# Differential attention with its outputs in two PSUM banks in turn, two casts in ten on ScalarE, and dense bias tables in layer 0

## The chip, the cores and the metric

The kernel is one program on one core of a Trainium2 chip. The metric is the device time of the whole program in microseconds (us), the median of three runs. A core has five engines that run at the same time and wait for each other through semaphores: TensorE (PE in the profile; its weight loads are PEld), VectorE (DVE), ScalarE (ACT), GpSimd (POOL) and SyncE (SP), whose queue issues nearly all transfers here. Each engine and each queue takes its instructions strictly in the order in which the program holds them, so an instruction that waits holds up all that stands behind it. TensorE runs at one of two clocks, 1.2 or 2.4 GHz; the profile's rows give the granted clock as a share of the higher one.

## What is computed

Two transformer layers over 1024 latent tokens (a 16 x 64 grid) and 256 context tokens, width 1024, all in 32-bit numbers. The parts that the change touches are these two.

```python
# layer 0, heads 0 to 7: neighbourhood attention with a bias by relative position
bias = jnp.take(col_bias, row_off, axis=1)
s_win = einsum(q_r, k_win) * scale + bias
p = softmax(concatenate([s_win, s_ctx]))
...
# layer 1, 8 heads of two maps each: differential attention
s1 = einsum('bhqd,bhkd->bhqk', a1, k1) * scale
s2 = einsum('bhqd,bhkd->bhqk', a2, k2) * scale
p = softmax(s1) - lam * softmax(s2)
o = einsum('bhqk,bhkd->bhqd', p, v)
y = merge_heads(rms_norm(o, subln_gain) * (1.0 - lambda_init)) @ w_out
```

Every layer also has six vectors of shift, scale and gate (`ada_params`): a vector of 1024 conditioning values times a 1024 x 6144 matrix, for the latent and for the context tokens.

## The kernel before

Each 32-bit matmul operand is split into a high and a low part (`hi`, `lo`), and a product is three matmuls (`mm3`, L181 to L183). Names in the rows: `psm` is a PSUM tile of a projection, `psq` one of the small PSUM tiles for maxima and sums, `pst` scores, `psv` a head's output.

**The projections of layer 0** (about 175 to 474 us in the trace). First the values for ten token groups, twice (L181 to L183 with `vwh`), then eight chunks `ch` of queries and keys, each 72 matmuls (`project`), whose results go through PSUM and are stored to HBM as high and low parts (`qh`, `ql`, `kh`, `kl`). Three things are laid between them:

- `maxima`: the largest score of every query of every head, which the later softmax subtracts. Each step is a matmul (L432) and a maximum on VectorE (L406, L410). A budget (`early`) lets 200 steps be recorded among the projections; the rest are recorded in the attention stage.
- `ada_acc` and `ada_sum`: eight loads of 512 KB (`aw`) for one of the six vectors, sixteen multiply-adds on VectorE into two accumulators (L210, L214), and then 16 one-column matmuls on TensorE (L235) that add up the accumulators over partitions: sixteen rows of the profile for each accumulator, since each 32-bit matmul shows as two. There are three such sets here; the sum of one frees the two accumulators for the next.
- `tables`: for each pair of heads and each of two orientations, the bias rows are loaded, GpSimd adds a mask (L631), and the result is stored to the HBM tensor `sk`. Each row of 127 values is copied for all 64 columns, and `skew` later reads the table from `sk` with a stride that is one less than its row, so that column c sees the window that begins at 63 - c. The pieces are 8 and 7 rows high and use the same three buffers (`aw`) as the loads of `ada_acc`.

The order on each engine is made by a scheduler, which follows the order of recording and a priority. What is recorded under `later()` has a lower priority: it is put behind other work that could go at the same time. All `ada_acc` sets and all `tables` here are recorded under it. What the scheduler takes to be early is a forecast, not a measured time.

**Attention of layer 0** (474 to 914 us) sums its scores with table rows loaded from `sk` (`key_table`, L877 adds them) and works through heads 8 to 15 and then 0 to 7.

**Differential attention** (2510 to 2815 us): 8 heads, two halves of 512 queries each, ten key chunks `kc` in a half. For one chunk TensorE makes two maps of scores (four matmuls, L1318 and L1319), ScalarE takes two exponentials (L1323, L1324), VectorE makes the difference (L1327) and its high part (L1328, the cast), and GpSimd or VectorE the low part (L1329). Six chunks later TensorE multiplies with the values: three matmuls into the half's output `po` (`pv`, L1290 to L1292). After the tenth chunk ScalarE copies `po` to SBUF (L1300) and squares it, and three chunks into the next half `gain` sums the squares over partitions with one matmul (L1248), takes the reciprocal root (`rsqrt`, L310 to L314) and scales the output. PSUM has eight banks, and all are taken:

```python
pst = ps("t", 3, 1024)        # 3 x 2 banks: scores
po = ps("v", VB1)             # 1 bank: output of a half
gain1(o, sq, None, qmt())     # 1 bank ("q"): sums of squares
```

The rest (output projections, feed-forward parts, projections of layer 1) is left as it is, apart from `rsqrt`, which every norm calls.

Of the kernel before, what the change touches and what calls it, by code (L numbers as in the profile page):

```python
# [23 lines left out]
NFF = 22  # L24
EPS = 1e-6
GW = 64
RPW = 127
RPN = 15 * RPW
# [6 lines left out]
QB1, VB1, LAG1 = 1, 1, 6  # L35
FAR1 = (0,1,2,3,4,5,6,7)
FARS, FARE, FARQ = 27, 108, .3
T5 = [8]
# [11 lines left out]


@with_exitstack
def kernel(ctx: ExitStack, tc: tile.TileContext, xT, cond, ada_w, ada_b, win0, wv0, wout0, rp, rpf, qg, kg,
                       win1, wv1, wout1, wg, wu, wd, lamv, subln, fgain, cosT, sinT, consts, cmT, cmQ, out):
    nc = tc.nc
    f = lambda ap: ap.bitcast(F32)
# [75 lines left out]
    sk = [dram([8, 64 * RPN + 2048], f"sk{i}") for i in range(2)]  # L132

    def small_operands():
        nc.sync.dma_start(slt, subln)
# [13 lines left out]
        nc.vector.tensor_scalar(slt, slt, 1.0 - LAMBDA_INIT, None, op0=ALU.mult)  # L149

    def skew(i, h, dr0, n):
        o = 63 + dr0 * RPW
        v = sk[i][h, o : o + 64 * (RPN - 1)].rearrange("(c n) -> c n", c=64)
        return v[:, : n * RPW].rearrange("c (u y) -> c u y", y=RPW)[:, :, :GW]


    pq = [None]
# [140 lines left out]
    def later():  # L298

        return tc.high_priority(-LATER)  # L300


    def rsqrt(pool, src, w, scale, bufs=None):

        if pool is None:
            a = wpool.tile([P, 1024], F32, tag="wh", bufs=4, name=nm("rs"))
            y, s = a[:, :w], a[:, 512 : 512 + w]
        else:
            y, s = (pool.tile([P, 512], F32, tag="tmp", bufs=bufs, name=nm("rs"))[:, :w] for _ in range(2))
        after_table(nc.scalar.activation(y, src, AF.Ln, bias=eps, scale=scale))  # L310
        last_ln[0] = after_table(nc.scalar.activation(y, y, AF.Exp, scale=-0.5))
        nc.scalar.activation(s, y, AF.Square, scale=math.sqrt(0.5 * scale))
        nc.vector.scalar_tensor_tensor(s, src, EPS / scale, s, op0=ALU.add, op1=ALU.mult)
        nc.vector.scalar_tensor_tensor(y, s, 1.5, y, op0=ALU.subtract, op1=ALU.mult, reverse0=True)  # L314
        return y

    def sumsq_add(pool, ssq, x, first, tag=("tmp", 512, 8), eng=None):
# [167 lines left out]
    with sbuf("hp0", 8) as hp, sbuf("a10", 8) as ap:  # L485
# [118 lines left out]
        for g in range(2):  # L604
# [15 lines left out]
        cmt = ap.tile([P, 2, RPW], F32, tag="cmt", bufs=1, name="cmt")  # L620

        def tables(i, h):

            for d0, d1 in ((0, 8), (8, 15)):
                n = d1 - d0
                T = ap.tile([P, 8, RPW], F32, tag="aw", bufs=3, name=nm("sk"))[:, 0:n, :]
                T2 = T.rearrange("p u y -> p (u y)")
                for j in range(2):
                    src = (rpf, rp)[i][h + j : h + j + 1, d0 * RPW : d1 * RPW].to_broadcast([64, n * RPW])
                    nc.sync.dma_start(T2[64 * j : 64 * j + 64], src)  # L630
                nc.gpsimd.tensor_add(T, T, cmt[:, i : i + 1, :].to_broadcast([P, n, RPW]))  # L631
                for j in range(2):
                    dst = sk[i][h + j, : 64 * RPN].rearrange("(c n) -> c n", c=64)[:, d0 * RPW : d1 * RPW]
                    nc.sync.dma_start(dst, T2[64 * j : 64 * j + 64])

        mpool = None
        tabs8 = [(i, h) for h in range(0, 8, 2) for i in range(2)]
# [77 lines left out]
        for ch in range(8):  # L715
            w = load_wchunk(win0[ch])
            hi, lo = t5(tpool), t5(tpool)
            for b, c0, cw, _ in BLK0:
                pst = mmt()[:, :cw]
                project(pst, w, hh[b], hl[b])  # L720
                early(VSHARE + (1 - VSHARE) * (ch * 1280 + c0 + cw) / 10240)
                put_plain(pst, hi[:, c0 : c0 + cw], lo[:, c0 : c0 + cw], 0.125 if ch < 4 else None)
            r = slice(P * (ch % 4), P * (ch % 4) + P)
            q = nc.gpsimd if ch > 6 else nc.sync
            q.dma_start((qh0, kh0)[ch // 4][r], f(hi))
            q.dma_start((ql0, kl0)[ch // 4][r], f(lo))
            if ch < 4:
                next_tables()
            if ch in (1, 4):
                ada_sum(*pend_ada, qmt)  # L730
            if ch == 1:
                with later():
                    pend_ada = ada_acc(ap, *adas.pop(0))

        stack0.close()

# [515 lines left out]

    mbufs[0], qb[0] = 6, QB1
    aT = [None] + [[btile(lpool, "hl", b, F32) for _ in range(KD)] for b in (1, 2)]
    with sbuf("a21") as ap, psum("pa21") as pq[0]:
        state = {}
# [25 lines left out]
        pend, norms, last = [], [], []  # L1284

        def pv():
            po, v, kc, hi, lo, o = pend.pop(0)
            if kc == 3 and norms:
                gain()
            nc.tensor.matmul(po, v[0][:, kc, :], hi, start=kc == 0, stop=False)  # L1290
            nc.tensor.matmul(po, v[1][:, kc, :], hi, start=False, stop=False)
            nc.tensor.matmul(po, v[0][:, kc, :], lo, start=False, stop=kc == 9)  # L1292
            if kc == 9 and not last:
                finish(po, o)
            elif kc == 9:
                nc.scalar.copy(o, po)
# [6 lines left out]
        def gain():  # L1303
            o, sq = norms.pop(0)
            gain1(o, sq, None, qmt())

        def attend1(hd):
            qs, ks, v = state.pop(hd)
            for hf in range(2):
                c0 = hf * 512  # L1310
                po = ps("v", VB1)

                for kc in range(10):
                    pst = ps("t", 3, 1024)
                    kk = slice(kc * P, kc * P + P)
# [12 lines left out]
                    nc.vector.tensor_copy(hi, p)  # L1328
                    (nc.vector if kc % 2 else nc.gpsimd).tensor_sub(lo, p, f(hi))  # L1329
                    pend.append((po, v, kc, hi, lo, aT[1 + hf][hd]))  # L1330
# [141 lines left out]
```

## Time and profile before

| | |
|---|---|
| median of 3 runs | 3656.18 us (3655.86 to 3661.64) |
| the profiled execution | 3658.97 us |
| its span, first to last instruction | 3657.2 us |
| busy: TensorE, VectorE, ScalarE, GpSimd | 3415.5, 2218.4, 1422.3, 825.2 us |
| mean granted clock of TensorE | 0.966 |

The span is the time from the first to the last instruction, and what lies around it is 1.8 us. A busy time is a sum over the span; matmuls follow each other in a pipeline and their rows overlap, so a start-to-start distance says more of TensorE than the length of a row.

### The profile page before, as it was taken

What the parts mean: (1) busy time and instruction counts of PE and PEld (TensorE: products, weight loads), DVE (VectorE), ACT (ScalarE), POOL (GpSimd) and SP (SyncE); (2) the same over time, 40 slices, a digit from 0 to 9 for tenths busy, and PEclk for the clock granted to TensorE, in tenths of its full rate; (3) what the DMA queues carried; (4) which work ended last, traced back from release to release, by engine and by line L of the source; (5) the groups of instructions that cost most, each with busy time, mean ns of one, the idle gap of its engine ahead of it and who ended that gap; (6) DMA issues with size and microseconds to landing.
All of it is one profiled execution on the core that took longest, in us unless ns stands there. A gap on an engine that the chain in (4) does not pass through costs nothing.

```text
span 3657.2 us, 43706 instructions
## 1 busy us (share of the span) xinstructions
PE 3415.5 (93%) x16044; PEld 2783.9 (76%) x16044; DVE 2218.4 (61%) x3555; ACT 1422.3 (39%) x2862; POOL 825.2 (23%) x622
## 2 busy tenths in 40 slices
PE   6799699988999999999998899899999999999997
PEld 4588577766888888888886678787666888888886
DVE  7767388887755555554336366787998533433335
ACT  4431067666441111111115254797777421111112
POOL 3212177766220000000003322002332200000002
PEclk8899789999999999999999999999999999999999
DMA  5276764374413333231112553646442211111111
GB/s 212 78 241 223 219 136 103 87 142 97 165 52 98 104 104 98 93 98 47 35 41 87 135 140 100 201 149 189 125 127 91 98 47 50 49 53 47 47 47 64
DMA packets 198081, 394.51 MB, mean 108 GB/s; under 512 B 57692, under 2 KB 99216, under 8 KB 197866
## 3 DMA queue, kind: packets, MB, share of 16 engines
q1 hardware_dynamic: 196074, 388.62, 36.0%
q0 software_dynamic: 1792, 3.10, 0.2%
q8 instruction: 126, 2.06, 0.2%
q14 instruction: 89, 0.73, 0.1%
HBM read 317.03 MB, written 74.61 MB: 107 GB/s over the span
## 4 chain that ended last, share of the span: by engine, by line
PE 74%; DVE 10%; ACT 5%; POOL 3%; issue 3%; DMA 3%; SPq 1%; POOLq 0%; DVEq 0%; ACTq 0%
PE psd L181 6%; PE psd L182 6%; PE psd L183 6%; PE psg L181 5%; PE psg L182 5%; PE psg L183 5%; PE psu L183 4%; PE psu L181 4%; PE psu L182 4%; PE psm L183 4%; PE psm L182 4%; PE psm L181 4%; PE pst L1318 2%; PE psq L1063 2%; PE pst L1319 2%
## 5 line engine op out<-in xcount | busy, mean ns | idle before, releaser
L173 POOL TENSOR_TENSOR wl<-wr,wh 128x1024 fp32r<-128x1024 f32 x69 | 168.0, 2435 | 1521.7 <-ACT wh L172 1315.4
L172 ACT CAST wh<-wr 128x1024 fp32r<-128x1024 f32 x193 | 202.2, 1049 | 761.7 <-PE psd L182 305.7
L993 DVE SCALAR_TENSOR_TENSOR x<-psd,mods,x 128x512 f32<-128x512 f32 (+1 forms) x448 | 301.3, 686 | 190.7 <-PE psd L183 190.4
L1027 DVE TENSOR_TENSOR sg<-sg,psu 128x512 f32<-128x512 f32 (+1 forms) x110 | 69.6, 634 | 484.4 <-PE psu L183 477.9
L181 PE MATMUL psd<-ah,wh 128*128 128x512 f32 (+1 forms) x896 | 331.3, 370 | 8.8 <-DVE x L993 6.8
L182 PE MATMUL psd<-al,wh 128*128 128x512 f32 (+1 forms) x896 | 328.3, 366 | 0.0
L183 PE MATMUL psd<-ah,wl 128*128 128x512 f32 (+1 forms) x896 | 326.9, 366 | 0.8 <-DVE wl L173 0.7
L181 PE MATMUL psg<-hh,wh 128*128 128x512 f32 (+1 forms) x880 | 326.2, 371 | 0.9 <-ACT sg L1024 0.9
L183 PE MATMUL psg<-hh,wl 128*128 128x512 f32 (+1 forms) x880 | 325.3, 370 | 0.1
L182 PE MATMUL psg<-hl,wh 128*128 128x512 f32 (+1 forms) x880 | 325.0, 369 | 0.0
L183 PE MATMUL psu<-hh,wl 128*128 128x512 f32 (+1 forms) x880 | 323.8, 368 | 0.5 <-POOL wl L173 0.5
L181 PE MATMUL psu<-hh,wh 128*128 128x512 f32 (+1 forms) x880 | 324.1, 368 | 0.0
L182 PE MATMUL psu<-hl,wh 128*128 128x512 f32 (+1 forms) x880 | 323.6, 368 | 0.0
L173 DVE TENSOR_TENSOR wl<-wr,wh 128x1024 fp32r<-128x1024 f32 x124 | 156.0, 1258 | 220.7 <-ACT wh L172 204.8
L1065 DVE TENSOR_REDUCE st<-psq 128x1 f32<-128x512 f32 (+1 forms) x384 | 219.4, 596 | 58.3 <-PE psq L1064 53.5
L1066 ACT ACTIVATE psq<-psq,st 128x512 f32<-128x512 f32 (+1 forms) x384 | 226.8, 594 | 65.0 <-DVE st L1065 61.3
L181 PE MATMUL psm<-hh,wh 128*128 128x512 f32 (+1 forms) x584 | 219.2, 376 | 25.7 <-ACT wh L172 18.4
L849 POOL TENSOR_TENSOR pl<-sb,ph 128x512 fp32r<-128x512 f32 (+1 forms) x144 | 203.5, 1420 | 91.9 <-ACT ph L848 60.2
L182 PE MATMUL psm<-hl,wh 128*128 128x512 f32 (+1 forms) x584 | 217.4, 373 | 6.5 <-DVE hl L349 4.7
L183 PE MATMUL psm<-hh,wl 128*128 128x512 f32 (+1 forms) x584 | 217.9, 373 | 3.7 <-POOL wl L173 3.7
L181 PEld LDWEIGHTS psd<-ah,wh 128*128 128x128 f32 x896 | 169.4, 189 | 44.0 <-DVE x L993 13.5
L1024 ACT ACTIVATE sg<-psg 128x512 f32<-128x512 f32 (+1 forms) x110 | 60.5, 552 | 344.4 <-PE psg L183 344.4
(276 smaller groups left out, 8331.2 us busy)
## 6 DMA issues: line engine op xcount, KB each, us to landing
aw<-in_ada_w SPq DMA_DIRECT2D x112, 512.0 KB
wr<-in_wg SPq DMA_DIRECT2D x44, 512.0 KB
wr<-in_wu SPq DMA_DIRECT2D x44, 512.0 KB
wr<-in_wd SPq DMA_DIRECT2D x44, 512.0 KB
k<-ks SPq DMA_DIRECT2D x32, 640.0 KB
wr<-in_wout SPq DMA_DIRECT2D x32, 512.0 KB
q<-qs SPq DMA_DIRECT2D x32, 512.0 KB
k<-ks SPq DMA_DIRECT2D x48, 320.0 KB
```

The source lines that it names most:

```text
L172: nc.scalar.copy(hi, raw)
L173: (eng or nc.gpsimd).tensor_sub(lo, raw, f(hi))
L181: nc.tensor.matmul(o, ah, bh, start=start, stop=False)
L182: nc.tensor.matmul(o, ah, bl, start=False, stop=False)
L183: nc.tensor.matmul(o, al, bh, start=False, stop=stop)
L849: (nc.vector if npb[0] % LOD == 0 else nc.gpsimd).tensor_sub(lo, e, f(hi))
L993: nc.vector.scalar_tensor_tensor(xv, pst, mods[:, l, ci, 40 + oc : 41 + oc], xv, op0=ALU.mult, op1=ALU.add)
L1063: nc.tensor.matmul(p1, q2[:, a * P : a * P + P], k2[:, k0 : k0 + kw], start=True, stop=False)
L1065: nc.vector.tensor_reduce(st[:, 0, a, j : j + 1], p1, axis=AX.X, op=ALU.max, negate=True)
L1066: after_table(nc.scalar.activation(p1, p1, AF.Exp, bias=st[:, 0, a, j : j + 1], accum_out=st[:, 1, a, j : j + 1]))
L1318: nc.tensor.matmul(o, ks[c][1][:, kk], qs[c][1][:, c0 : c0 + 512], start=True, stop=False)
L1319: nc.tensor.matmul(o, ks[c][0][:, kk], qs[c][0][:, c0 : c0 + 512], start=False, stop=True)
```

## The change

Five edits. (1) In differential attention the two single banks `v` and `q` become `v0` and `v1`: half n writes its output into bank n mod 2, and the sum of squares of half n goes into that same bank later. (2) For chunks 3 and 7 of ten the cast to the high part is made on ScalarE in place of VectorE. (3) The bias tables come dense from the host, one row of 64 values for each column (`tabT`, `tabQ`); one load, one add and one store per head pair and orientation, over 128 partitions and all 15 rows, and `skew` is a plain slice. (4) In the projections of layer 0 the third `ada_acc` is no longer recorded under `later()`, and its `ada_sum` is recorded at chunk 6 in place of chunk 4. (5) `rsqrt` writes its product in place over its source in PSUM, where before it went to SBUF.

```diff
-            for d0, d1 in ((0, 8), (8, 15)):
-                n = d1 - d0
-                T = ap.tile([P, 8, RPW], F32, tag="aw", bufs=3, name=nm("sk"))[:, 0:n, :]
-                T2 = T.rearrange("p u y -> p (u y)")
-                for j in range(2):
-                    src = (rpf, rp)[i][h + j : h + j + 1, d0 * RPW : d1 * RPW].to_broadcast([64, n * RPW])
-                    nc.sync.dma_start(T2[64 * j : 64 * j + 64], src)
-                nc.gpsimd.tensor_add(T, T, cmt[:, i : i + 1, :].to_broadcast([P, n, RPW]))
-                for j in range(2):
-                    dst = sk[i][h + j, : 64 * RPN].rearrange("(c n) -> c n", c=64)[:, d0 * RPW : d1 * RPW]
-                    nc.sync.dma_start(dst, T2[64 * j : 64 * j + 64])
+            T = ap.tile([P, 15, GW], F32, tag="aw", bufs=3, name=nm("sk"))
+            r = slice(64 * h, 64 * h + P)
+            nc.sync.dma_start(T.rearrange("p u y -> p (u y)"), (tabT, tabQ)[i][r])
+            nc.gpsimd.tensor_add(T, T, cmt[:, i : i + 1, :].to_broadcast([P, 15, GW]))
+            nc.sync.dma_start(sk[i][r], T.rearrange("p u y -> p (u y)"))
...
     def skew(i, h, dr0, n):
-        o = 63 + dr0 * RPW
-        v = sk[i][h, o : o + 64 * (RPN - 1)].rearrange("(c n) -> c n", c=64)
-        return v[:, : n * RPW].rearrange("c (u y) -> c u y", y=RPW)[:, :, :GW]
+        return sk[i][64 * h : 64 * h + 64, dr0 * GW : (dr0 + n) * GW].rearrange("c (u y) -> c u y", y=GW)
...
-            if ch in (1, 4):
+            if ch in (1, 6):
                 ada_sum(*pend_ada, qmt)
             if ch == 1:
-                with later():
-                    pend_ada = ada_acc(ap, *adas.pop(0))
+                pend_ada = ada_acc(ap, *adas.pop(0))
...
-        nc.vector.scalar_tensor_tensor(s, src, EPS / scale, s, op0=ALU.add, op1=ALU.mult)
-        nc.vector.scalar_tensor_tensor(y, s, 1.5, y, op0=ALU.subtract, op1=ALU.mult, reverse0=True)
+        nc.vector.scalar_tensor_tensor(src, src, EPS / scale, s, op0=ALU.add, op1=ALU.mult)
+        nc.vector.scalar_tensor_tensor(y, src, 1.5, y, op0=ALU.subtract, op1=ALU.mult, reverse0=True)
...
-                gain()
+                gain(n - 1)
...
+        def bank(n):
+            return ps(f"v{n % 2}", 1)
...
-            gain1(o, sq, None, qmt())
+            gain1(o, sq, None, bank(n))
...
-                po = ps("v", VB1)
-
+                n = 2 * hd + hf
+                po = bank(n)
...
-                    nc.vector.tensor_copy(hi, p)
+                    if kc in (3, 7):
+                        nc.scalar.copy(hi, p)
+                    else:
+                        nc.vector.tensor_copy(hi, p)
```

TensorE at the end of the layer 0 projections, before: `psm` with three matmuls is the last of chunk 7, `acc` the third set of `ada_acc`.

```order
L181 MATMUL psm_3628<-hh_537,wh_3533 128x512
L182 MATMUL psm_3628<-hl_538,wh_3533 128x512
L183 MATMUL psm_3628<-hh_537,wl_3532 128x512
L235 MATMUL psq_3216<-cst,acc_2710 128x1 x8
L432 MATMUL psq_3268<-km_1342,qm_2877 128x512
L432 MATMUL psq_3271<-km_1342,qm_2877 128x256
L235 MATMUL psq_3216<-cst,acc_2711 128x1 x8
```

TensorE in the change, in the first and second block of chunk 7:

```order
L178 MATMUL psm_3475<-hh_303,wh_3469 128x256
L179 MATMUL psm_3475<-hl_304,wh_3469 128x256
L180 MATMUL psm_3475<-hh_303,wl_3468 128x256
L429 MATMUL psq_3500<-km_1341,qm_3288 128x512
L429 MATMUL psq_3503<-km_1341,qm_3288 128x512
L178 MATMUL psm_3511<-hh_430,wh_3469 128x512
L179 MATMUL psm_3511<-hl_431,wh_3469 128x512
L232 MATMUL psq_3448<-cst,acc_2663 128x1 x8
L180 MATMUL psm_3511<-hh_430,wl_3468 128x512
L178 MATMUL psm_3511<-hh_436,wh_3469 128x512
L429 MATMUL psq_3506<-km_1341,qm_3288 128x256
```

The two groups of one-column matmuls stood behind the last projection matmul, ahead of 52 steps of `maxima` (L432) and of the attention. They now stand inside chunk 7, and 43 of those 52 steps stand among the projection matmuls; 9 are left between the last projection matmul and the first of the attention. The matmuls ahead of the attention are the same in kind and number.

The SP queue around the third set of `ada_acc` loads, before: `t` are operands of the first attention heads, `sk` the tables, and the eight loads begin behind them.

```order
L767 DMA t_743_3775<-qh_86 64x1280
L768 DMA t_742_3774<-qh_86 64x1280
L769 DMA t_742_3774<-qm_88 1x1280
L766 DMA t_840_4115<-ql_87 64x1280
L767 DMA t_840_4115<-qh_86 64x1280
L768 DMA t_839_4114<-qh_86 64x1280
L769 DMA t_839_4114<-qm_88 1x1280
L634 DMA sk_99<-sk_2679 64x1016
L634 DMA sk_99<-sk_2685 64x889 x2
L207 DMA aw_2712<-in_ada_w 128x1024
L207 DMA aw_2716<-in_ada_w 128x1024
```

The SP queue in the change, where those eight loads stand now: between the stores of chunk 1 (`ql_87<-t_479`) and of chunk 2 (`ql_87<-t_519`).

```order
L717 DMA ql_87<-t_479_2499 128x1280
L625 DMA sk_99<-sk_2338 128x960
L623 DMA sk_2488<-in_tabT 128x960
L623 DMA sk_2639<-in_tabQ 128x960
L204 DMA aw_2664<-in_ada_w 128x1024
L625 DMA sk_98<-sk_2488 128x960
L625 DMA sk_99<-sk_2639 128x960
L204 DMA aw_2668<-in_ada_w 128x1024
L204 DMA aw_2672<-in_ada_w 128x1024
L204 DMA aw_2676<-in_ada_w 128x1024
L421 DMA km_1342<-kh_89 64x1280
L204 DMA aw_2680<-in_ada_w 128x1024
```

Five of the eight loads are among these rows. They moved ahead of the stores of chunks 2 to 7 and of the operands of the attention. A head pair in one orientation now has two table transfers in this queue, where it had eight.

ScalarE in differential attention in the change, from a `gain` to one of the two casts of a half (L1317 and L1318 are the exponentials that were L1323 and L1324):

```order
L307 ACTIVATE rs_21674<-psv_4111_21672,eps 128x512
L308 ACTIVATE rs_21674<-rs_21674 128x512
L1317 ACTIVATE e_21616<-pst_21611 128x512
L309 ACTIVATE rs_21674<-rs_21674 128x512
L1318 ACTIVATE pst_21611<-pst_21611 128x512
L1317 ACTIVATE e_21632<-pst_21627 128x512
L1318 ACTIVATE pst_21627<-pst_21627 128x512
L1317 ACTIVATE e_21648<-pst_21643 128x512
L1318 ACTIVATE pst_21643<-pst_21643 128x512
L1317 ACTIVATE e_21664<-pst_21659 128x512
L1323 CAST ph_21636<-pst_21627 128x512
L1318 ACTIVATE pst_21659<-pst_21659 128x512
```

The cast of `pst_21627` stands three exponentials behind the one that made its input (`pst_21627`), so the difference on VectorE falls in between. Before, ScalarE had no row but exponentials, copies, squares and the three of `rsqrt` here.

## Rows read from the trace of the kernel before

**Rows 1.** The page: the span, and busy time of each engine

```profile
span 3657.2 us, 43706 instructions
...
PE 3415.5 (93%) x16044; PEld 2783.9 (76%) x16044; DVE 2218.4 (61%) x3555; ACT 1422.3 (39%) x2862; POOL 825.2 (23%) x622
```

**Rows 2.** Windows: length, then busy time (instructions) by engine, TensorE's clock, DMA share, GB/s

```profile
225.00:405.30 180.30, 175.49 (x958) 153.56 (x957) 109.89 (x204) 32.31 (x92) 44.07 (x23) 0.93 0.69 216
405.30:439.00 33.70, 0.02 (x1) 0.00 (x0) 17.88 (x17) 0.58 (x1) 1.14 (x2) 0.55 0.81 255
439.00:474.20 35.20, 32.53 (x86) 21.80 (x87) 27.49 (x55) 0.53 (x2) 10.45 (x13) 0.50 0.62 166
474.20:914.00 439.80, 399.41 (x1832) 308.99 (x1830) 368.48 (x672) 313.52 (x588) 309.18 (x266) 0.98 0.52 109
...
2510.00:2815.00 305.00, 284.16 (x1147) 210.80 (x1147) 277.08 (x444) 219.34 (x396) 104.51 (x83) 1.00 0.44 124
```

**Rows 3.** Timeline of TensorE, 404.8 to 476: start, length, line, count, idle before

```profile
404.70 0.39 PE L182 MATMUL psm<-hl,wh 128*128 128x512 f32 x1
404.93 0.39 PE L183 MATMUL psm<-hh,wl 128*128 128x512 f32 x1
439.01 3.57 PE L235 MATMUL psq<-cst,acc 128*128 128x1 f32 x16 [33.69 <-DVE acc L214]
...
446.50 6.32 PE L432 MATMUL psq<-km,qm 128*128 128x512 f32 x12
...
474.25 0.41 PE L853 MATMUL pst<-t,t 128*128 128x256 f32 x1
```

**Rows 4.** The chain that ended last, 404 to 475, in order of time

```profile
419.23 3.89 DMA aw<-in_ada_w
...
455.55 12.68 DVE mx L410 x24
```

**Rows 5.** Timeline of the SP queue, 355 to 475

```profile
413.95 2.00 SPq L634 DMA_DIRECT2D sk<-sk  x3
416.00 17.27 SPq L207 DMA_DIRECT2D aw<-in_ada_w  x8
```

**Rows 6.** Timeline of TensorE, 326.5 to 338

```profile
326.87 1.95 PE L235 MATMUL psq<-cst,acc 128*128 128x1 f32 x16 [0.77 <-DVE acc L214]
...
330.06 3.39 PE L235 MATMUL psq<-cst,acc 128*128 128x1 f32 x16
333.31 0.77 PE L183 MATMUL psm<-hh,wl 128*128 128x512 f32 x1
...
336.66 0.51 PE L432 MATMUL psq<-km,qm 128*128 128x512 f32 x1
```

**Rows 7.** Timeline of TensorE, 2591 to 2611, one half head

```profile
2591.19 0.50 PE L1290 MATMUL psv<-ph,v 128*128 128x512 f32 x1 [1.12 <-ACT hl L1300]
...
2597.14 1.02 PE L1248 MATMUL psq<-o,cst 128*128 128x512 f32 x2
...
2608.76 0.39 PE L1292 MATMUL psv<-pl,v 128*128 128x512 f32 x1
2610.27 0.50 PE L1290 MATMUL psv<-ph,v 128*128 128x512 f32 x1 [1.12 <-ACT hl L1300]
```

**Rows 8.** Groups of instructions by line and shape, 2490 to 2830

```profile
L1290 PE MATMUL psv<-ph,v 128*128 128x512 f32 x160 | 64.6, 403 | 17.3 <-ACT hl L1300 16.6 <-DVE ph L1328 0.6
...
L1328 DVE CAST ph<-pst 128x512 fp32r<-128x512 f32 x80 | 54.9, 686 | 6.4
...
L314 DVE SCALAR_TENSOR_TENSOR rs<-rs 128x512 f32<-128x512 f32 x15 | 21.6, 1440 | 0.0
...
L1300 ACT COPY hl<-psv 128x512 f32<-128x512 f32 x15 | 8.9, 592 | 0.0
```

**Rows 9.** Waits of TensorE, 474 to 914: us in total, times, longest

```profile
PE psv L888 <- DVE rc L904: 8.2, 5, 2.6
...
PE psv L888 <- ACT ph L848: 0.2, 1, 0.2
```

More of the change, by code (lines that the diff above doesn't have):

```diff
@@ L26 @@
 GW = 64
-RPW = 127
-RPN = 15 * RPW
 NEG = -1e30
@@ L34 @@
 QB, VB, TB, X0, LOD = 3, 2, 3, 9, 4
-QB1, VB1, LAG1 = 1, 1, 6
+LAG1 = 6
 FAR1 = (0,1,2,3,4,5,6,7)
@@ L52, with kernel @@
 @with_exitstack
-def kernel(ctx: ExitStack, tc: tile.TileContext, xT, cond, ada_w, ada_b, win0, wv0, wout0, rp, rpf, qg, kg,
+def kernel(ctx: ExitStack, tc: tile.TileContext, xT, cond, ada_w, ada_b, win0, wv0, wout0, tabT, tabQ, qg, kg,
                        win1, wv1, wout1, wg, wu, wd, lamv, subln, fgain, cosT, sinT, consts, cmT, cmQ, out):
@@ L131 @@
     onesrow = dram([2, NT], "onesrow")
-    sk = [dram([8, 64 * RPN + 2048], f"sk{i}") for i in range(2)]
+    sk = [dram([8 * 64, 15 * GW], f"sk{i}") for i in range(2)]
     def small_operands():
@@ L619 @@
                 gqa_q(g, w1, w2, o, blk)
-        cmt = ap.tile([P, 2, RPW], F32, tag="cmt", bufs=1, name="cmt")
+        cmt = ap.tile([P, 2, GW], F32, tag="cmt", bufs=1, name="cmt")
         def tables(i, h):
-            for d0, d1 in ((0, 8), (8, 15)):
-                n = d1 - d0
-                T = ap.tile([P, 8, RPW], F32, tag="aw", bufs=3, name=nm("sk"))[:, 0:n, :]
-                T2 = T.rearrange("p u y -> p (u y)")
-                for j in range(2):
-                    src = (rpf, rp)[i][h + j : h + j + 1, d0 * RPW : d1 * RPW].to_broadcast([64, n * RPW])
-                    nc.sync.dma_start(T2[64 * j : 64 * j + 64], src)
-                nc.gpsimd.tensor_add(T, T, cmt[:, i : i + 1, :].to_broadcast([P, n, RPW]))
-                for j in range(2):
-                    dst = sk[i][h + j, : 64 * RPN].rearrange("(c n) -> c n", c=64)[:, d0 * RPW : d1 * RPW]
-                    nc.sync.dma_start(dst, T2[64 * j : 64 * j + 64])
+            T = ap.tile([P, 15, GW], F32, tag="aw", bufs=3, name=nm("sk"))
[3 more added lines that the diff above has]
+            nc.sync.dma_start(sk[i][r], T.rearrange("p u y -> p (u y)"))
         mpool = None
@@ L1250, in gain1 @@
         nc.vector.scalar_tensor_tensor(o, o, slt[:, 0:1], rstd, op0=ALU.mult, op1=ALU.mult)
-    mbufs[0], qb[0] = 6, QB1
+    mbufs[0] = 6
     aT = [None] + [[btile(lpool, "hl", b, F32) for _ in range(KD)] for b in (1, 2)]
@@ L1286, in pv @@
         def pv():
-            po, v, kc, hi, lo, o = pend.pop(0)
+            po, v, kc, hi, lo, o, n = pend.pop(0)
             if kc == 3 and norms:
-                gain()
+                gain(n - 1)
             nc.tensor.matmul(po, v[0][:, kc, :], hi, start=kc == 0, stop=False)
@@ L1301, in finish, with gain @@
             norms.append((o, square1(o, wpool.tile([P, 1024], F32, tag="wh", bufs=4, name=nm("o"))[:, :512])))
-        def gain():
+        def bank(n):
+            return ps(f"v{n % 2}", 1)
+        def gain(n):
             o, sq = norms.pop(0)
-            gain1(o, sq, None, qmt())
+            gain1(o, sq, None, bank(n))
         def attend1(hd):
@@ L1327, in attend1 @@
                     nc.vector.scalar_tensor_tensor(p, e2, nlam, e1, op0=ALU.mult, op1=ALU.add)
-                    nc.vector.tensor_copy(hi, p)
+                    if kc in (3, 7):
+                        nc.scalar.copy(hi, p)
+                    else:
+                        nc.vector.tensor_copy(hi, p)
                     (nc.vector if kc % 2 else nc.gpsimd).tensor_sub(lo, p, f(hi))
-                    pend.append((po, v, kc, hi, lo, aT[1 + hf][hd]))
+                    pend.append((po, v, kc, hi, lo, aT[1 + hf][hd], n))
                     if len(pend) > LAG1:
@@ L1409 @@
     rp = np.pad(inp["na_rpb"][0], ((0, 0), (0, 0), (48, 48)))
+    x = GW - 1 - np.arange(GW)[:, None] + np.arange(GW)[None, :]
+    tabQ, tabT = (t[:, :, x].transpose(0, 2, 1, 3).reshape(8 * GW, 15 * GW) for t in (rp, rp[:, ::-1, ::-1]))
     qgain, kgain = inp["gqa_q_gain"][0], inp["gqa_k_gain"][0]
@@ L1425 @@
     inside = (c[None, :] >= start[:, None]) & (c[None, :] < start[:, None] + 16)
-    x = np.arange(RPW)
-    kc = np.clip(c[:, None] + x[None, :] - 63, 0, GW - 1)
-    mq = np.where(inside[c[:, None], kc], f32(0), f32(NEG)).astype(f32)
-    qc = np.clip(c[:, None] + x[None, :] - 63, 0, GW - 1)
-    mt = np.where(inside[qc, c[:, None]], f32(0), f32(NEG)).astype(f32)
-    cmT, cmQ = np.concatenate([mt, mt], axis=0), np.concatenate([mq, mq], axis=0)
+    mq = np.where(inside, f32(0), f32(NEG)).astype(f32)
+    cmT, cmQ = np.concatenate([mq.T, mq.T], axis=0), np.concatenate([mq, mq], axis=0)
     arrays = dict(
@@ L1441 @@
         wout0=chunks(inp["par_w_out"][0], np.arange(D)),
-        rp=rp.reshape(8, RPN), rpf=rp[:, ::-1, ::-1].reshape(8, RPN),
+        tabT=tabT, tabQ=tabQ,
         qg=np.stack([np.tile(qgain[0::2], 4), np.tile(qgain[1::2], 4)], axis=1),
```

## Prediction

> **What bounds the kernel now.** I read the page first. TensorE is busy for 3415.5 of 3657.2 us [rows 1], so the kernel is TensorE's, and a change gains only where TensorE stands idle or runs at its lower clock. I then looked for the windows in which it does so and lie in code that the diff touches. There are two.
>
> The first is the end of layer 0's projections [rows 2]. From 405.3 to 439.0 TensorE is busy for 0.02 of 33.7 us, and from 439.0 to 474.2 it is busy but at a granted clock of 0.50, which is 1.2 GHz. TensorE's timeline shows why [rows 3]: the last projection matmul starts at 404.93, the next instruction is the one-column sum of the third adaLN set, and it waits 33.69 us for the accumulator on VectorE. Behind it stand 52 steps of maxima, and only at 474.25 does the attention begin. The chain of work that ended last goes through a load of `aw` at 419.23 and later through 24 maxima on VectorE in 12.68 us, 0.53 each [rows 4]. The SP queue names the first link: the eight loads of the set are issued from 416.00, behind table stores at 413.95 [rows 5]. So TensorE stands behind a sum that no matmul of this stage uses, because its loads were queued last.
>
> The second is differential attention, where TensorE is busy for 284.16 of 305 us [rows 2]. Once in a half head, 15 times, the first matmul into `po` waits for ScalarE's copy out of the one bank, 16.6 us in all by the groups [rows 8]. On the timeline of one half, which lasts from 2591.19 to 2610.27, that is 19.08 us, the matmul before starts at 2608.76 [rows 7]. Matmuls of 512 columns start 0.23 apart [rows 3], so the hole is 2610.27 - 2608.99 = 1.28 us. The row says 1.12 because its neighbour's end is modelled.
>
> **The change part by part.**
>
> *The third set goes ahead, its sum into chunk 7.* The 33.7 us wait goes, and so does the bare stretch behind it. From the end of the last projection matmul (404.93 + 0.23) to the attention it was 474.25 - 405.16 = 69.1 us. The same matmuls now cost:
> - the two sums among full matmuls. The second set shows this [rows 6]: one group takes 1.95, the other 3.25 (330.06 to 333.31), and the matmuls after it run at half speed until 336.66, which loses half of 3.35, 1.7. Together 6.9 us.
> - 43 maxima steps among the projections. Two of three have 512 columns (0.23), one 256 (half of that): 0.19 on average, 8.2 us.
> - the 9 steps that stay bare, at VectorE's pace of 0.53 [rows 4]: 4.8 us.
>
> The sum is 19.9, the gain 49.2 us. It rests on VectorE keeping up. Its work from 225 to 474 is 109.9 + 17.9 + 27.5 = 155.3 us [rows 2]; this now has about 200 us and not 249, 78% and not 62%. In the attention of layer 0, where VectorE is at 84% (368.48 of 439.80), TensorE idles 9.2%; in the projections it idles 2.7% (175.49 of 180.30). If the projections became as bad as the attention, 6.5% of 200 us would come back, 13 us; if VectorE kept up, nothing. I take 3, since 78% is short of 84%. **Gain 46 us, bounds 36 to 49.**
>
> *Dense tables.* By the shapes in the diff a head pair's table shrinks from 128 x 1905 to 128 x 960 values, for the load, the add and the store, and eight transfers become two. For eight tables that is some 7.7 MB less out and in, 36 us of transfers at 216 GB/s [rows 2]. On the path this is nothing by itself: where tables are made TensorE was 97% busy (175.49 of 180.30), and the one place that waited on their queue is counted above. In the attention the loads from `sk` become long runs, but TensorE's twelve kinds of waits there are all for VectorE, GpSimd or ScalarE, from 8.2 us down to 0.2 [rows 9]. I take nothing; the bounds are 0 and 10 us of gain, a quarter of its 40 us of idle time there.
>
> *Two banks in turn.* The first matmul of a half needs the bank of the half before the last, whose sum of squares was read three chunks into the last half, seven chunks earlier. The 1.28 us hole goes: 15 x 1.28 = 19.2 us. What else a half has over its matmuls is 19.08 - 1.28 - 70 x 0.23 - 1.0 (the sum of squares at 2597.14 [rows 7]) = 0.7 us of waits, most of them for VectorE. If those went too, the gain would be 15 x 1.98 = 30 us.
>
> *Two casts on ScalarE.* Both chunks are odd, so the source is in PSUM: VectorE loses two casts of 0.686 a half [rows 8]. ScalarE gets two; its nearest row is the copy of 128x512 out of PSUM, 0.592 [rows 8]. ScalarE is busy for 219.34 of 305 us [rows 2], 13.7 of a half's 19.08. With the casts it is 14.9, against 17.1 of matmuls. Behind each cast stand exponentials, for whose scores TensorE's next tile waits; but the cast stands three exponentials behind its input's, so the difference on VectorE (about 0.7 us) should be done. I let what VectorE gives back and what ScalarE's queue costs cancel: **gain 19 us, bounds 4 to 30.**
>
> There is a rule against this edit. The Trainium skill, ScalarE: Activation LUTs, Rules for kernel authors, sends simple elementwise work to VectorE, which it calls up to about 3 times faster (for 16-bit data). This trace has 0.592 on ScalarE beside 0.686 on VectorE for 32-bit data out of PSUM, so it does not bear that out. By the rule the casts would be 2.06 each as an estimate, ScalarE 17.8 a half and without slack; that is the case C below.
>
> *`rsqrt` in place.* The second step read two halves of one SBUF tile in the 15 `gain` calls and took 1.440 [rows 8]; now one operand is in PSUM, and I expect about half. That is 10 us less on VectorE, hidden behind TensorE. For the other norms I take nothing; some eight of them have TensorE waiting, at half a microsecond either way that is 4 us.
>
> Sum: 46 + 19 = 65 us off the profiled execution's 3658.97, 3594. The median lies 2.8 below that execution, so 3591 in its terms.
>
> **The rivals.**
>
> *B, part of the stall comes back elsewhere.* The set's loads wait for buffers that tables hold, and the second set's sum also moves forward; if either sum meets an accumulator that is not ready, TensorE waits in chunk 2 or 7. For it: transfers are busy at 0.69 of their capacity there [rows 2], and the same sort of wait cost 33.7. Against it: in the rows of the order the third set's loads stand around chunk 1's stores and its sum in chunk 7, five chunks of 72 matmuls, over 80 us, for what took 439.0 - 416.0 = 23 us [rows 3, 5]. Half the wait back, 17 us: 3608; all of it: 3625. Chance 0.14.
>
> *C, ScalarE sets the pace of differential attention.* Its exponentials then come late by a part of each cast's wait, and 1 us of the 1.28 returns in each half. For it: its queue is strictly in order. Against it: each cast would have to cost over (17.1 - 13.7) / 2 = 1.7 us. Gain there 4 and not 19: 3606. Chance 0.12.
>
> *D, the attention of layer 0 gains too*, since table loads no longer crowd the queue: 10 us more, and a bit of VectorE's slack in differential attention: 3578. Against it: TensorE waits for no transfer there [rows 9]. The Trainium skill, DMA: Bandwidth & Descriptors, Specifications, wants at least 512 bytes in a run for full rate, and the old reads have 256; no run here shows yet what that is worth. Chance 0.06.
>
> *E, slower.* Each of the 32 casts holds ScalarE until VectorE, behind with other chunks, has made the difference, and the three score tiles run full. From 65 / 32 = 2.0 us a cast all is eaten; at 2.4 it is 77 us, 3668. Against it: the distance of three exponentials, and a VectorE that is relieved of 1.4 + 0.7 us a half. Chance 0.04.
>
> *F, the wait is only renamed*, with SP's queue as full as before and no gain: about 3654. Against it: the order. Chance 0.02.
>
> **How the numbers follow.** The forecast, A, has 0.62 and its own range from 3577 (gains of 49 and 30) to 3605. The range of 3569 to 3622 adds most of D's 10 us below, and C and all but the worst of B above; E, F and B's tail are left out, about 0.1, and sizes that I missed as much again. Faster and slower begin at 0.2%, 7 us, about what a measurement of this kernel tells from no change. Faster: A to D, 0.94; same: F, 0.02; slower: E, 0.04.
>
> **What would show it.** Right: no wait of over 5 us by a one-column sum after 300 us; the attention's first matmul (now L843) at about 428 (474.25 - 46), with the clock near 1.0 ahead of it; no wait of `pv` (now L1280) for the copy (now L1290), and halves of about 17.8 us; the rest of the kernel as long as before. Wrong: a one-column sum that waits in chunk 2 or 7 (B); halves still near 19 with TensorE waiting for the casts or exponentials (C, E); an attention of layer 0 that is not 440 us long within 5 (D, or VectorE's work moved into it).

## The result and the profile after

The changed kernel takes 3600.89 us in the median of four runs (3599.16 to 3608.6) beside 3658.68 before: a ratio of 0.9846, 95% interval 0.9828 to 0.9864, or 58 us less. The profiled execution is the longest of the four, 3608.6. A second profile of the same kernel (the control below) has a span of 3600.7; where the two differ, both numbers are given.

The page, span and busy time, for [rows 1]:

```profile
span 3606.8 us, 43538 instructions
...
PE 3403.7 (94%) x16044; PEld 2780.2 (77%) x16044; DVE 2193.5 (61%) x3523; ACT 1435.9 (40%) x2894; POOL 811.7 (23%) x614
```

The windows that answer to [rows 2]: projections up to chunk 7, their end, attention of layer 0, differential attention. Columns as there.

```profile
225.00:394.20 169.20, 155.70 (x833) 134.70 (x832) 136.82 (x227) 29.64 (x86) 40.50 (x20) 0.91 0.62 213
394.20:436.20 42.00, 41.16 (x224) 34.34 (x222) 23.64 (x50) 4.22 (x9) 2.99 (x10) 1.00 0.63 179
436.20:879.90 443.70, 403.29 (x1832) 314.11 (x1832) 370.64 (x673) 312.92 (x589) 310.33 (x267) 0.97 0.47 115
2475.00:2771.80 296.80, 286.39 (x1150) 211.24 (x1150) 258.29 (x416) 234.44 (x431) 104.64 (x83) 1.00 0.47 130
```

The empty stretch and the half-clock stretch are gone: up to the attention the clock is 1.00 and TensorE busy for 41.16 of 42 us. TensorE's timeline there, for [rows 3]: the attention begins at 436.15 and not at 474.25, with waits for maxima of half a microsecond at most ahead of it.

```profile
432.53 0.74 PE L429 MATMUL psq<-km,qm 128*128 128x512 f32 x3
433.70 0.71 PE L429 MATMUL psq<-km,qm 128*128 128x512 f32 x2 [0.43 <-DVE mx L407]
434.63 1.44 PE L429 MATMUL psq<-km,qm 128*128 128x512 f32 x4 [0.22 <-DVE mx L407]
436.15 0.39 PE L843 MATMUL pst<-t,t 128*128 128x256 f32 x1
```

SP's queue, for [rows 5]: the loads of the third set (three rows, eight loads with one at 322) are issued by 351, the last table is stored at 367. Before, the last loads went at 433 and the last table stores at 463.9.

```profile
335.68 1.28 SPq L204 DMA_DIRECT2D aw<-in_ada_w  x3
343.20 0.33 SPq L204 DMA_DIRECT2D aw<-in_ada_w  x1
...
345.59 5.11 SPq L204 DMA_DIRECT2D aw<-in_ada_w  x3
...
367.11 2.55 SPq L625 DMA_DIRECT2D sk<-sk  x2
```

Differential attention by groups, first two rows of before that stand beside those of [rows 8]:

```profile
L1318 PE MATMUL pst<-q,k 128*128 128x512 f32 x320 | 130.0, 407 | 4.8 <-DVE pl L1329 1.9 <-DVE vl L357 1.3 <-DVE e L1327 0.9
L1250 DVE SCALAR_TENSOR_TENSOR hl<-hl,slt,rs 128x512 f32<-128x512 f32 x15 | 11.8, 787 | 0.0
```

In the change, `pv` (L1280) no longer waits for the copy, 16.6 us before; the waits at the scores rise from 4.8 to 7.4 us. A half is 18.3 us (the copies of the halves start from 2497.88 to 2754.41, 14 steps) where it was 19.1.

```profile
L1312 PE MATMUL pst<-q,k 128*128 128x512 f32 x320 | 134.5, 421 | 7.4 <-DVE e L1321 5.7 <-DVE vl L354 1.3 <-DVE pl L1326 0.4
L1280 PE MATMUL psv<-ph,v 128*128 128x512 f32 x160 | 63.9, 400 | 1.6 <-DVE ph L1325 1.2 <-ACT ph L1323 0.4
L1240 DVE SCALAR_TENSOR_TENSOR hl<-hl,slt,rs 128x512 f32<-128x512 f32 x16 | 21.7, 1354 | 0.0
L1323 ACT CAST ph<-pst 128x512 fp32r<-128x512 f32 x32 | 18.8, 588 | 0.0
L311 DVE SCALAR_TENSOR_TENSOR rs<-psv,rs 128x512 f32<-128x512 f32 x15 | 10.2, 682 | 0.0
```

### The profile page after: what moved, and what is told of

Read it like the earlier page. It is cut to its first block, busy times and chain, and to the rows that moved or that the text cites. A ratio compares the mean times of both kernels' runs of the same rounds, so it can differ in the third digit from the quotient of the medians.

```text
span 3606.8 us, 43538 instructions
## 1 busy us (share of the span) xinstructions
PE 3403.7 (94%) x16044; PEld 2780.2 (77%) x16044; DVE 2193.5 (61%) x3523; ACT 1435.9 (40%) x2894; POOL 811.7 (23%) x614
## 4 chain that ended last, share of the span: by engine, by line
PE 74%; DVE 10%; ACT 4%; POOL 3%; issue 3%; DMA 3%; SPq 0%; POOLq 0%; ACTq 0%; DVEq 0%
PE psd L178 6%; PE psd L179 6%; PE psd L180 6%; PE psg L178 5%; PE psg L179 5%; PE psg L180 5%; PE psu L180 5%; PE psu L178 5%; PE psu L179 5%; PE psm L180 4%; PE psm L179 4%; PE psm L178 4%; PE pst L1312 2%; PE psq L1053 2%; PE psq L1054 2%
```

## The experiments

Twelve kernels in three groups; each group has its own runs of the kernel before on its chip (medians 3659.1, 3657.8 and 3661.1 us), and the ratio is to those. The stages are from one profile each: to the first score matmul of layer 0's attention, the part of it that begins with the first matmul of the chunks of queries and keys, from the first score matmul of layer 0's attention to its output projection, and from the first score matmul of differential attention to its output projection (us).

| kernel | median | ratio, 95% interval | to attention 0 | of it, chunks | attention 0 | diff. attention |
|---|---|---|---|---|---|---|
| before | | | 474.3 | 204.4 | 440.1 | 308.5 |
| change | 3600.9 | 0.9846 (0.9828 to 0.9864) | 436.2 | 161.5 | 443.7 | 296.7 |
| change, control | 3602.0 | 0.9834 (0.9820 to 0.9847) | 434.8 | 160.4 | 441.2 | 296.7 |
| edit 4 alone | 3658.6 | 1.0002 (0.9992 to 1.0011) | 445.3 | 178.6 | 468.6 | 308.4 |
| tables alone | 3608.0 | 0.9864 (0.9850 to 0.9879) | 428.7 | 155.0 | 439.2 | 308.2 |
| tables alone, in pieces | 3629.7 | 0.9908 (0.9895 to 0.9922) | 428.3 | 159.6 | 460.3 | 308.4 |
| two banks alone | 3657.5 | 0.9997 (0.9987 to 1.0007) | 472.2 | 206.5 | 439.8 | 307.8 |
| casts alone | 3664.1 | 1.0016 (1.0006 to 1.0025) | 473.4 | 206.3 | 442.2 | 313.1 |
| change without edit 4 | 3593.8 | 0.9821 (0.9806 to 0.9835) | 430.5 | 156.2 | 440.6 | 296.6 |
| change without casts | 3607.8 | 0.9860 (0.9843 to 0.9876) | 431.6 | 160.3 | 440.7 | 305.5 |
| change, `rsqrt` not in place | 3603.9 | 0.9850 (0.9835 to 0.9864) | 432.7 | 160.8 | 440.6 | 301.1 |
| change, `rstd` in PSUM | 3595.4 | 0.9827 (0.9812 to 0.9842) | 430.3 | 161.4 | 441.3 | 290.3 |
| the same without edit 4 | 3593.2 | 0.9816 (0.9803 to 0.9829) | 428.1 | 155.5 | 443.2 | 290.4 |
| and with a third cast | 3599.4 | 0.9830 (0.9816 to 0.9843) | 428.7 | 155.0 | 443.1 | 294.8 |

Differential attention repeats within 0.3 us among kernels that have the same code there (308.2 to 308.5, 296.6 to 296.7, 290.3 to 290.4). The start of attention 0 does not: the chunks of queries and keys begin anywhere from 265.6 to 274.7 us, by up to 5.8 us apart where TensorE's order up to there is the same. So what an edit does in these chunks is read from their own column.

### Which edit ends the stall of layer 0

**Edit 4 alone**, on the kernel before.

```diff
-            if ch in (1, 4):
+            if ch in (1, 6):
                 ada_sum(*pend_ada, qmt)
             if ch == 1:
-                with later():
-                    pend_ada = ada_acc(ap, *adas.pop(0))
+                pend_ada = ada_acc(ap, *adas.pop(0))
```

> The kernel before with edit 4 alone (third set not recorded as later, its sum recorded at chunk 6). Theory 1, as in the prediction: edit 4 by itself brings the gain of layer 0, 38 us in the profiled executions, so the time is near 3620 us and the first matmul of attention 0 starts at about 436 us. Rival: the order of the loads is set by the queue that the old tables fill. In this kernel's order the eight loads still stand behind the tables and behind the stores of chunk 7, and the sum stands behind the last projection matmul, so most of the 33.7 us wait stays; only about 30 maxima steps move ahead of it, at most 8 to 16 us. By the rival the time is 3640 to 3656 us and a one-column sum still waits 20 us or more.

The rival is the nearer one, though by another route than it gave: the time, 3658.6, lies just past its range, and the sum waits 17.6 us. The attention begins 29 us earlier and then lasts 28.5 us longer; the time is that of before. TensorE's timeline of this kernel:

```profile
428.69 3.57 PE L235 MATMUL psq<-cst,acc 128*128 128x1 f32 x16 [17.58 <-DVE acc L214]
433.12 3.41 PE L235 MATMUL psq<-cst,acc 128*128 128x1 f32 x16
445.27 0.41 PE L852 MATMUL pst<-t,t 128*128 128x256 f32 x1
...
474.61 0.79 PE L852 MATMUL pst<-t,t 128*128 128x512 f32 x1 [15.34 <-ACT sb L842]
```

Half of the old wait is left at the sum, and a new one of 15.34 stands in the attention, for ScalarE. ScalarE waits for GpSimd's low parts (`pl`, L848), and those stand behind the mask on a table (L631). ScalarE and GpSimd, then SP:

```profile
473.96 2.50 ACT L842 ACTIVATE sb<-pst 128x512 f32<-128x512 f32 x4 [15.74 <-POOL pl L848]
```

```profile
452.94 4.02 POOL L631 TENSOR_TENSOR sk<-sk,cmt 128x1016 f32<-128x1016 f32 x2 [0.27 <-DMA sk<-in_rpf]
...
467.36 4.05 POOL L631 TENSOR_TENSOR sk<-sk,cmt 128x1016 f32<-128x1016 f32 x2 [9.84 <-issue]
```

```profile
420.01 3.10 SPq L207 DMA_DIRECT2D aw<-in_ada_w  x2
...
459.15 6.47 SPq L630 DMA_DIRECT2D sk<-in_rp  x4
469.55 2.98 SPq L634 DMA_DIRECT2D sk<-sk  x4
```

The row of GpSimd's 9.84 us names no releaser; the first two of the four table loads (L630) that it needs were issued at 459.15 and 460.15, so a transfer fits. Loads and tables share a queue and three buffers: the loads went earlier, so the last tables went later, stored until 472.5 where it was 463.9.

**Dense tables alone** (the change with all other edits undone; the diff is edit 3 as shown above).

> The changed kernel with every edit undone but the dense tables (edit 3). Theory 1, as in the prediction: dense tables are worth nothing on the path, so the time is that of before within 10 us, 3646 to 3660. Rival: with a quarter of the table transfers the eight loads move up in SP's queue by themselves (in this kernel's order they stand around the stores of chunks 2 and 3 though still recorded as later, and the sum stands in chunk 4 or 5 among full matmuls), and the stall goes: 3616 to 3624 us, attention 0 begins at about 436 us.

The rival held, with more than it expected: 51 us by the medians. Attention 0 begins 45.6 us earlier (474.3 to 428.7), and the chunks alone are 49.4 us shorter. The spans of the two profiles differ by 54.3 us; 7.6 of it lie in stages ahead of and behind differential attention whose code is the same. The third set is still recorded as `later`, yet its loads now go by 365 and its sum runs among full matmuls. SP and TensorE of this kernel:

```profile
333.27 0.33 SPq L204 DMA_DIRECT2D aw<-in_ada_w  x1
339.29 12.34 SPq L204 DMA_DIRECT2D aw<-in_ada_w  x4
361.30 3.87 SPq L204 DMA_DIRECT2D aw<-in_ada_w  x2
381.19 2.66 SPq L625 DMA_DIRECT2D sk<-sk  x2
```

```profile
379.40 0.39 PE L179 MATMUL psm<-hl,wh 128*128 128x512 f32 x1
379.63 1.84 PE L232 MATMUL psq<-cst,acc 128*128 128x1 f32 x16
```

**Dense tables in pieces**: as many table transfers and buffer turns as before, but half the bytes.

```diff
-            T = ap.tile([P, 15, GW], F32, tag="aw", bufs=3, name=nm("sk"))
-            r = slice(64 * h, 64 * h + P)
+            for d0, d1 in ((0, 8), (8, 15)):
+                n = d1 - d0
+                T = ap.tile([P, 8, GW], F32, tag="aw", bufs=3, name=nm("sk"))[:, 0:n, :]
...
+                for j in range(2):
+                    r = slice(64 * h + 64 * j, 64 * h + 64 * j + 64)
+                    nc.sync.dma_start(sk[i][r, d0 * GW : d1 * GW], T2[64 * j : 64 * j + 64])
```

> The kernel with dense tables alone, in which each table is again cut into pieces of 8 and 7 rows with a transfer for each of two heads: as many table transfers and buffer turns as before the change, but the dense bytes. Theory 2a, the bytes are what filled the transfers: near the 3608 us of the dense tables alone, 3604 to 3614, attention 0 begins at 428 to 434 us. Theory 2b, the number of transfers and of turns through the three buffers is what matters: half of the 51 us or more is lost, 3630 to 3658 us, and a one-column sum of the third set waits 15 us or more.

Between both. The projections keep nearly the whole gain (attention 0 begins at 428.3, the chunks are 4.6 us longer than with whole tables), and 20 us go in the attention (460.3), where TensorE is at a mean clock of 0.82 from 428 to 480. The last table stores are late again: they stand behind loads of `km` in SP's queue, and behind them stand the loads of `v`, for which TensorE waits.

```profile
404.77 0.47 SPq L631 DMA_DIRECT2D sk<-sk  x1
...
438.00 0.45 SPq L421 DMA_DIRECT2D km<-kh  x1
...
440.01 1.75 SPq L631 DMA_DIRECT2D sk<-sk  x3
441.80 2.28 SPq L781 DMA_DIRECT2D v<-vs  x2
```

```profile
449.65 0.58 PE L885 MATMUL psv<-ph,v 128*128 128x256 f32 x1 [2.75 <-DMA v<-vs]
```

So with half the bytes in as many transfers the projections are nearly free of the stall. But the eight loads also stand earlier in the queue than before (issued at 357 to 384 us and not at 416 to 433), so that bytes and order are not told apart. The rest of the gain needs fewer pieces, or the order that comes with them; which of these two it is was not tried.

**The change without edit 4** (the reverse of the diff above).

> The changed kernel with edit 4 alone undone (third set recorded as later, its sum at chunk 4). Theory 2, after the first four runs: the tables' transfers and the third set's loads share SP's queue and three buffers, and whichever goes first delays the other; with dense tables there is room for both, and edit 4 is worth nothing or a little less than nothing: 3593 to 3602 us, attention 0 begins at 428 to 437 us. Theory 1, as in the prediction: the earlier place of the loads is needed, and a part of the stall comes back: 3610 to 3640 us.

Theory 2 held: no part of the stall comes back. With the control:

> The changed kernel once more, as a control beside the next three. If its late start of attention 0 (436.2 us, where four later variants with the same projections have 428.7 to 432.7) belongs to that one execution, the start is 428 to 433 us here and the time 3594 to 3603 us; if edit 4 makes it, it is 436 again.

The control begins attention 0 at 434.8, so the late start is not that one execution's alone. The column of the chunks tells what edit 4 does beside dense tables: they take 160.3 to 161.5 us in the five kernels that have both, and 155.0 to 156.2 in the four with whole dense tables and without edit 4. In each of the five, and in none of the four, TensorE waits 3.1 to 3.9 us for a maximum at 353 to 359 us, while VectorE works through six multiply-adds of the third set in a row (L211), and the granted clock falls to 0.50 around it. In the change:

```profile
359.04 0.39 PE L429 MATMUL psq<-km,qm 128*128 128x256 f32 x1 [3.63 <-DVE mx L407]
```

Edit 4 thus costs about 5 us of this stage once the tables are dense. The medians go the same way, 7 to 8 us apart, and 2 for the two with `rstd` in PSUM, but in both pairs the intervals overlap.

### Banks, casts and `rsqrt` in differential attention

**Two banks alone**, on the kernel before.

```diff
+        def bank(n):
+            return ps(f"v{n % 2}", 1)
...
-            gain1(o, sq, None, qmt())
+            gain1(o, sq, None, bank(n))
...
-                po = ps("v", VB1)
+                n = 2 * hd + hf
+                po = bank(n)
```

> The kernel before with the two banks alone (edit 1). Theory 1: the one bank is what a half waits for, 1.28 us of each of 15 halves, and the casts cancel, so the gain is that of both edits together, about 12 us as in the profiled execution of the change, and up to 19: 3640 to 3648 us; no wait of the values' first matmul for the copy. Rival: without the casts on ScalarE, VectorE (busy for 277 of 305 us before) becomes the next wait and takes most of it: gain 0 to 5 us, 3652 to 3659 us, with TensorE waiting for the difference or the casts for over 1 us a half.

The rival held: 0.7 us of 308.5, and 1.2 by the medians. The 16.6 us of waits for the copy are gone, and others of the same size have taken their place. TensorE's waits of this kernel (us in total, times, longest):

```profile
PE psv L1292 <- POOL pl L1333: 6.1, 16, 0.6
PE pst L1322 <- DVE pl L1333: 5.5, 14, 0.5
PE pst L1322 <- DVE e L1331: 5.3, 7, 0.9
...
PE psv L1291 <- DMA v<-vs: 1.6, 2, 1.4
```

VectorE is busy for 277.9 us of this stage, 17.4 a half, against 17.1 of matmuls, and works in a fixed order. Read from one half (2600 to 2622 us) and not tested by itself: where its 2.9 us of `gain` fall (0.69, 1.49 and 0.74), the low parts and the score tiles come late.

**Two casts alone**, on the kernel before.

```diff
-                    nc.vector.tensor_copy(hi, p)
+                    if kc in (3, 7):
+                        nc.scalar.copy(hi, p)
+                    else:
+                        nc.vector.tensor_copy(hi, p)
```

> The kernel before with two of ten casts on ScalarE alone (edit 2). Theory 1: the hole of 1.28 us a half stays, since the one bank is still read by the copy, and the casts are hidden: 3656 to 3662 us. Rival: VectorE's relief of 1.4 us a half shortens the halves by itself: gain of 5 to 12 us, 3646 to 3653 us. A second rival: the casts hold up the exponentials and the copy, which the hole waits for: 3664 us or more.

The second rival's size, 3664.1, but not its path: the stage is 4.6 us longer. The wait for the copy is all there, VectorE itself now waits for the casts, and TensorE's wait for the low parts at the scores rises from 1.9 to 6.6:

```profile
DVE pl L1332 <- ACT ph L1329: 37.1, 31, 1.2
...
PE psv L1290 <- ACT hl L1300: 16.8, 15, 1.1
...
PE pst L1318 <- DVE pl L1332: 6.6, 14, 0.5
```

The low part of an odd chunk (L1332, on VectorE) needs the high part, so a cast that ScalarE makes late stops VectorE for 1.2 us, more than the 0.69 that it saves. In the change the same wait is 6.1 us in 14 times.

**The change without casts** (all ten on VectorE, two banks kept).

> The changed kernel with all ten casts back on VectorE (edit 2 undone). Theory 2: with two banks VectorE is the next bound of a half (277.6 us of work in 307 us with the two banks alone), so the gain of differential attention needs the relief of the casts; the stage goes back to 305 to 308 us and the time to 3609 to 3613 us. Rival: the two banks alone failed for another reason (the old rsqrt, or the order), and here the stage stays within 3 us of the 296.7 of the change: 3599 to 3604 us.

Theory 2 held in size: 305.5, with the time, 3607.8, just short of its range. But 5.0 us of it are three waits of `pv` for loads of `v`, which no other kernel here has in that size; so the casts are worth 4 to 9 us beside two banks, and 4.6 less than nothing beside one.

**`rsqrt` not in place** (the reverse of edit 5).

> The changed kernel with rsqrt not in place (edit 5 undone). Theory: the time of one VectorE step of the 15 gain calls only moves (its 1.44 us came back in the scaling of the output, which reads two SBUF operands as well), so the edit is worth nothing: 3598 to 3604 us, and the second step of rsqrt is 1.4 us again while the scaling falls to about 0.75. Rival: in the change VectorE is close to the bound of a half, and 0.7 us there is worth up to 10 us: 3605 to 3611 us.

The time agrees with the theory, the stage is 4.4 us longer, and the sizes are neither's: the second step has a mean of 0.897 and the scaling 1.234. VectorE's total is the same 258.2 us as in the change. A wait that the change does not have, 3.2 us in three times, stands at the matmul of the sums, for the square on ScalarE. Why it does so here is open.

**`rstd` in PSUM**: in the 15 `gain` calls the last step of `rsqrt` goes to the bank too.

```diff
+        if keep:
+            y0, y = y, src
+        else:
+            y0 = y
-        nc.vector.scalar_tensor_tensor(y, src, 1.5, y, op0=ALU.subtract, op1=ALU.mult, reverse0=True)
+        nc.vector.scalar_tensor_tensor(y, src, 1.5, y0, op0=ALU.subtract, op1=ALU.mult, reverse0=True)
```

> The changed kernel, in which rsqrt of the 15 gain calls also leaves its result in the PSUM bank, so that the scaling of the output reads one operand from PSUM and one from SBUF. Theory: the doubled time comes from two SBUF operands beside a GpSimd instruction that reads SBUF; then the scaling takes 0.7 us in place of a mean of 1.35, VectorE loses 10 us in the stage, and since VectorE is near its bound 2 to 6 us of it are gained: 3595 to 3599 us. Rival 1: the operands have nothing to do with it, the scaling stays at 1.4. Rival 2: it falls and the time stays within 2 us, since a half then waits for something else.

The theory held. The scaling takes 0.741 in place of 1.354, VectorE 248.5 in place of 258.2, and the stage 6.4 us less. Groups of this kernel:

```profile
L1244 DVE SCALAR_TENSOR_TENSOR hl<-hl,slt,psv 128x512 f32<-128x512 f32 x15 | 11.1, 741 | 0.0
L315 DVE SCALAR_TENSOR_TENSOR psv<-psv,rs 128x512 f32<-128x512 f32 x15 | 10.4, 693 | 0.0
```

**The same without edit 4, and then with a third cast.**

> The changed kernel without edit 4, and with the result of rsqrt left in PSUM in the 15 gain calls. If edit 4 costs nothing and brings nothing, this is the run with rsqrt in PSUM again: 3592 to 3598 us. If edit 4 costs the 4 to 7 us by which the medians of the run without it lay lower: 3586 to 3591 us. Differential attention takes 290 us within 2 in both.

> The kernel of the run before this one with a third cast on ScalarE (chunk 1 as well). Theory 2: VectorE's work sets the length of a half, about 0.6 us of the stage for each us of VectorE (277.9 to 307.8, 269.4 to 305.5, 258.2 to 296.7, 248.5 to 290.3); 11 us less of it give 5 to 7 us, the stage takes 283 to 286 us, the time falls by 4 to 7 us against the run before. Rival, case C of the prediction: ScalarE, at 15.2 us of 17.1 in a half, now holds up its exponentials, and the stage is as long or longer, 290 us or more. Second rival: TensorE's own matmuls, 281.6 us busy, are nearly all that is left, and the gain is 0 to 3 us.

The first is the fastest kernel found, 3593.15 us, 0.9816 of before, as its first case has it; its interval overlaps those of its two neighbours. With the third cast the stage is 4.4 us longer, far more than it varies, and the median 6 us higher, though these two intervals overlap. So its first rival has it, though the exponentials are not what waits. VectorE is: it makes 32 casts out of PSUM for 22.0 us in place of 48 for 33.0, and its waits for ScalarE's casts rise from 6.0 to 21.4.

```profile
DVE pl L1331 <- ACT ph L1328: 21.4, 27, 1.2
```

## Why the prediction was right, and where not

The total was right (65 us forecast, 58 measured by the medians), and the two stages that were to gain did, within their bounds. The reasons were half wrong, and that the total came out in spite of it is in part luck: the gain credited to edit 4 is that of edit 3, and the change happens to hold both.

**The stall of layer 0.** That TensorE stood behind a sum whose loads were queued last, and what its end is worth, was right: 46 forecast, 38.1 and 39.4 in the two profiles of the change, 45.6 with the tables alone. Within the chunks of queries and keys it is 43.0 and 44.0, and 49.4 with the tables alone, so the sum of 49.2 was good. Those chunks begin at 274.7 and 274.4 us in the change and at 269.8 before; no run shows why. The step that failed is *the dense tables: "I take nothing"*. I counted "the one place that waited on their queue" with edit 4. But edit 4 alone leaves half of the wait and moves the other half into the attention, and dense tables alone end it. I had their 36 us of transfers, and priced them by TensorE's idle time where tables are made, and not by what stood behind them in the queue. The term for VectorE, 3 us, is 5 to 6 in the change: TensorE waits for maxima for 7.7 us in nine times, beside 3.7 in six with the tables alone, and most of the difference is the one wait that edit 4 brings.

**Rivals B and F** named the right danger (the loads wait for buffers that tables hold). It does not come in the change, and comes in full with edit 4 alone. **D** did not come: attention 0 takes 443.7 and 441.2 us, not less than 440.1. **C** and **E** did not come: in the change TensorE waits for ScalarE's casts for 0.4 us in all. The upper end of A's own range, 3605, stands without a sum; the bounds of 36 and 4 would give 3616.

**Two banks and casts.** The hole was 16.6 us by the waits and did close. Of the 19 us forecast 11.8 came, and halves of 18.3 and not 17.8. The step that failed is *the casts "cancel", and the banks bring the 19*: the banks alone bring 0.7, the casts alone cost 4.6, both together give 11.8 (with edit 5, worth up to 4.4 of it). VectorE, busy for 280 of 308.5 us before, had more work than TensorE's matmuls (16 halves of 17.1 are 274), so it had little time to give when the bank came free. That VectorE's time counts there is shown by `rstd` in PSUM: 9.7 us less on VectorE, 6.4 less in the stage. Its total is not the whole of it: `rsqrt` not in place leaves the total and adds 4.4, and the third cast takes 7.1 off it and adds 4.4. For the casts I looked at the exponentials behind them on ScalarE, and not at the low part behind them on VectorE.

**`rsqrt` in place.** "10 us less on VectorE" failed in the change, whose 258.2 us are also those of the run without edit 5: the step fell from 1.440 to 0.682 as expected, and the scaling rose from 0.787 (the mean of L1250 before) to 1.354. Without the casts 8.4 us did come off VectorE (277.9 to 269.4).

What stays open: the later begin of the chunks in the change; whether bytes or order free them; the waits for `v` without casts; and 3 to 4 us in the rest of the program after differential attention (838.4 before, 834 to 835.5 in most kernels with dense tables, 838 in two of them), which the total includes and the forecast did not.

## What to carry to other kernels

Before crediting a gain to the edit that moves a waiting load, ask what fills the queue ahead of it: here moving the load passed half of the wait to what it overtook, and taking work out of the queue ended it. A freed wait was worth what the next engine had to spare, so two edits that were each worth nothing paid together; run each alone and both. When a step moves to another engine, follow its result to the next reader, not only the queue that it joins.

## What the runs showed of the hardware

One VectorE form takes 0.73 or 1.44 us by what GpSimd does meanwhile. VectorE and GpSimd in one half before, where L314 and L1250 both read two SBUF tiles:

```profile
2603.37 1.43 DVE L314 SCALAR_TENSOR_TENSOR rs<-rs 128x512 f32<-128x512 f32 x1
...
2605.33 0.73 DVE L1250 SCALAR_TENSOR_TENSOR hl<-hl,slt,rs 128x512 f32<-128x512 f32 x1
```

```profile
2602.97 1.29 POOL L1329 TENSOR_TENSOR pl<-e,ph 128x512 fp32r<-128x512 f32 x1 [2.57 <-DVE ph L1328]
```

L314 overlaps the GpSimd instruction, L1250 does not. The other calls agree: of the steps L314 and L1250 before and L1240 in the change, in differential attention, the 30 that overlap a GpSimd instruction take 1.42 to 1.49 us, and the 18 that do not take 0.68 to 0.74. In the change the one that is left meets it: the scaling (L1240) starts at 2584.14 and takes 1.44, while GpSimd's runs from 2583.73 to 2585.02. With one operand in PSUM the same step has a mean of 0.741, though 14 of its 16 calls run wholly beside a GpSimd instruction. The Trainium skill, SBUF — State Buffer, Who interferes with whom, says that a VectorE instruction with two SBUF inputs contends with a GpSimd instruction that reads SBUF, and that one with at most one SBUF input does not, outside of two modes that it names. The runs agree with both.
